# A float32 attention layer on one core: inputs laid out in load order, x loaded transposed, scores of two head pairs at a time, high and low parts as neighbours

## Chip, cores and metric

One core of a Trainium2 chip runs the whole kernel. The metric is the device time of one execution in microseconds; for the kernel before it is the median of three runs, 153.05 (151.89 to 153.78). The host's rearranging of the arrays, ahead of the launch, is outside that time in both kernels.

## The reference

One layer (DEPTH = 1) of attention with a gate, then a root-mean-square norm, in float32, for 256 positions, 16 heads of 64 and a width of 1024. There is one key block of 256 positions, so the block selection of the reference never selects anything, and what is computed is causal attention with a linear distance penalty:

```python
h = rms_norm(x, norm_g)                       # x: 1 x 256 x 1024
q, k, v, gate = split(h @ w_in, 4)            # w_in: 1024 x 4096
s = q @ k.T * 64 ** -0.5 - slope[head] * (t_query - t_key)
s = where(t_key <= t_query, s, -inf)
o = softmax(s) @ v
x = x + (o * silu(gate)) @ w_out              # w_out: 1024 x 1024
return rms_norm(x, final_g)
```

## The kernel before

**Three products for one.** TensorE's fast float32 form (fp32r) keeps fewer bits, so every large product is made of three: each operand a is split into a high part (ACT copies it to fp32r) and a low part (DVE subtracts the high part from a), and high x high, low x high and high x low are added up in one PSUM bank. PEld in the profile is PE's loading of the weight that each matmul has.

**Stages.** The rows of x are in two blocks of 128 (m = 0, 1), the width in eight slices of 128 (k). `w_in` comes in pieces of 512 KB through four buffers, and its columns are projected in parts, in the order of the table `PARTS` (line 28): first half of v, then q, k, gate parts of 256 columns, among them the second half of v as the tenth part, and `w_out` last in eight pieces. A part of q, k or gate holds two head pairs; it takes 8 slices x 2 pairs x 3 matmuls of 256 columns. A part of v takes 8 x 2 x 3 of 512 columns. The norm's factor for each row (`rstd`) is not put into x but into the results, when they leave PSUM.

**The opening** (lines 172 to 179 and 501 to 640). SP issues half a row block of x, the first weight piece in two halves, half of the other row block, and so on. PE transposes x by a product with an identity (`x_tr`, line 519), ACT or DVE evacuate it with the gain into high parts (`x_evac`, line 523), DVE makes the low parts, and the 48 matmuls of the first half of v follow (`run_first`, line 594). Five matmuls on zeros (`warm`, line 496) fill PE before data are there; they wait for a memset on DVE. The 16 tables of the distance penalty (`make_bias`, line 211) are made 7 on DVE and 9 on ACT. Squares of x are summed on ACT (`square`, line 504) between the evacuations, and POOL raises them to the power -0.5 (line 514).

**Attention** (`fiber_pair`, line 317), for each of the 8 head pairs: 12 score matmuls of 64 rows into two PSUM banks, one for each head; for both query blocks DVE adds the penalty and takes the row's maximum in one operation (line 360), ACT takes the exponential with the sums; DVE scales by the reciprocal; PE transposes the probabilities, ACT and DVE split them (`pth`, `ptl`); three matmuls of 512 columns and three of 256 multiply them with the high and low v of both heads of the pair (`vh`, `vl`); DVE multiplies by the gate (line 433), ACT and DVE split the result (`oh`, `ol`).

**What sets the order.** All engines' instructions stand in the order in which Python writes them. A planner (`Plan`, line 53) keeps an estimated clock for each engine with costs for each kind of operation; the projections are written in a loop, and after every matmul `fill` (line 261) may add the splitting of a weight piece, and `side` (line 292) may add a step of one of the "fibers" (a pair's attention, an evacuation) whose inputs are due by the planner's clock. Eight PSUM banks are handed out by `take` and `give`; a projection of two pairs takes two. DMAs of weights are issued on SP as soon as a buffer's low part has been made.

**The end.** Out of the output projection the two row blocks come one after the other; each is added to x, squared, scaled by its factor on ACT and DVE, and leaves in two DMAs on SP (lines 722 to 752).

Of the kernel before, what the change touches and what calls it, by code (L numbers as in the profile page):

```python
# [13 lines left out]
P = 128  # L14
S = 256
# [12 lines left out]
PARTS = [("v", 0), ("q", 0), ("k", 0), ("g", 0), ("q", 1), ("k", 1), ("g", 1), ("q", 2), ("k", 2), ("v", 1),  # L28
         ("q", 3), ("k", 3), ("g", 2), ("g", 3)]
# [4 lines left out]
NKB = 3  # L34
# [8 lines left out]
WARM = 4  # L43
SPREAD = 200.0
WARM2 = 1
NB_DVE = 7
NB_ACT = 3
COLD = 6800.0
NL = 4
# [27 lines left out]
def trunk(ctx: ExitStack, tc, x, norm_g, w_in, w_out, fin_g, out):  # L77
# [9 lines left out]
    qp = ctx.enter_context(tc.tile_pool(name="qp", bufs=4))  # L87
    khp = ctx.enter_context(tc.tile_pool(name="khp", bufs=NKB))
    zp = ctx.enter_context(tc.tile_pool(name="zp", bufs=3))
# [4 lines left out]
    def mm(o, a, b, start, stop, n, dep=0.0):  # L94
        nc.tensor.matmul(o, a, b, start=start, stop=stop)  # L95
        return plan.mm(n, dep)
# [39 lines left out]
    g8 = const.tile([NK, P], F32, name="g8")  # L136
    nc.scalar.dma_start(g8, norm_g.rearrange("(a b) -> a b", b=P))

    x_at = [[0.0, 0.0], [0.0, 0.0]]
    w32, whi, wlo, w_at, w_ready = {}, {}, {}, {}, {}  # L140
    dma = [1680.0]

    def load_x(m, h):
        nc.sync.dma_start(xs[m][:, h * CW:(h + 1) * CW], x[0, m * P:(m + 1) * P, h * CW:(h + 1) * CW])  # L144
        dma[0] += 728.0
        x_at[m][h] = dma[0] + LAT

    def piece_src(i):

        if i < N_IN:  # L150
            kind, j, h = PIECES[i]
            w = CW if kind == "v" else GW
            r = KP * GW // w * P
            return w_in[h * r:(h + 1) * r, COL[kind] + j * w:COL[kind] + (j + 1) * w].rearrange("(a p) n -> p a n", p=P)
        k = i - N_IN
        return w_out[k * P:(k + 1) * P, :].rearrange("p (a n) -> p a n", n=CW)

    def load(i, parts=1, dep=0.0):
        if i >= N_PIECES:
            return  # L160
        w32[i] = w32p.tile([P, KP * GW], F32, name="w32")
        src = piece_src(i)
        a = src.shape[1]
        dst = w32[i].rearrange("p (a n) -> p a n", a=a)
        for u in range(parts):
            us = slice(u * a // parts, (u + 1) * a // parts)
            nc.sync.dma_start(dst[:, us, :], src[:, us, :])  # L167
        s = max(dma[0], dep)
        w_at[i] = [s + LAT + 1456.0 * (u + 1) / parts for u in range(parts)]
        dma[0] = s + 1456.0  # L170

    load_x(0, 0)
# [601 lines left out]
```

## Time and profile before

| | |
|---|---|
| median of 3 runs | 153.05 us |
| profiled execution, its own time | 154.04 us |
| its span, first to last instruction | 152.3 us |
| instructions | 2760 |
| granted TensorE clock, mean | 0.990 |
| DMA moved | 23.78 MB, mean 156 GB/s |

A row of the timeline is: start, duration, engine, line of the kernel, operation, what it writes and reads with the shape, how often it is repeated there, and in brackets the idle time before it and what ended that. A row of a window is: the window, its length, then for each engine the busy time and the number of instructions, the granted clock, the share of the DMA engines' time, and GB/s. A group's row is: what it is, the number, the busy time, the mean in ns of one, and the idle time ahead. Durations of matmuls overlap, so the distance of starts tells what one costs. The profiled execution lies 1.0 us above the median.

### The profile page before, as it was taken

Reading aid. Unit: us, or ns where it says so; the run is one execution under the profiler, and the core shown is the slowest. Engines: PE = TensorE matmul, PEld = TensorE weight load, DVE = VectorE, ACT = ScalarE, POOL = GpSimd, SP = SyncE. Lnnn points to the kernel's source line nnn. Section 1 sums busy time; section 2 is a strip of 40 time slices with the busy share of each in tenths; the row PEclk is TensorE's granted clock in tenths of the full one; section 3 lists DMA queues with packets and bytes.
Section 4 is the critical chain, followed back from the end, with each engine's and each line's share of the span. In section 5 each row is a group of like instructions: output and inputs, shape, how many; then the busy total and the mean of one; then the engine's idle time right before and its main releaser. Section 6 shows DMA issues by size and latency. Waiting matters only on the chain.

```text
span 152.3 us, 2760 instructions
## 1 busy us (share of the span) xinstructions
PE 143.6 (94%) x1008; PEld 129.7 (85%) x1008; DVE 118.7 (78%) x294; ACT 89.6 (59%) x199; POOL 4.1 (3%) x13
## 2 busy tenths in 40 slices
PE   6699999999999999999999999999999999999940
PEld 3388789999999998999997879999899988888830
DVE  5574897596899989898987799767686999674880
ACT  6375997546697443975744878464296493331231
POOL 3000010000000000000000000000000000000210
PEclk9999999999999999999999999999999999999995
DMA  4999479969704454231747605486430406100033
GB/s 142 260 359 338 137 206 265 340 176 279 241 27 138 138 180 158 80 123 31 264 146 210 201 1 154 132 285 235 167 138 4 138 0 229 46 2 4 11 127 138
DMA packets 17390, 23.78 MB, mean 156 GB/s; under 512 B 856, under 2 KB 13408, under 8 KB 17376
## 3 DMA queue, kind: packets, MB, share of 16 engines
q1 hardware_dynamic: 17216, 23.07, 47.1%
q10 hardware_dynamic: 160, 0.53, 1.4%
q8 instruction: 8, 0.13, 0.4%
q14 instruction: 6, 0.05, 0.1%
HBM read 22.55 MB, written 1.05 MB: 155 GB/s over the span
## 4 chain that ended last, share of the span: by engine, by line
PE 87%; DMA 4%; issue 3%; DVE 1%; SPq 1%; POOL 1%; ACT 0%; POOLq 0%
PE bank L95 78%; PE bank L99 5%; PE bank L343 4%; DMA x<-in_x 4%; POOL fr L745 1%; SPq L167 1%; DVE bias L736 0%; ACT bias L747 0%; POOLq L770 0%; DVE x L734 0%; SPq L144 0%; DVE fms L736 0%
## 5 line engine op out<-in xcount | busy, mean ns | idle before, releaser
L95 PE MATMUL bank<-xl,whi 128*128 128x256 f32 x192 | 55.0, 287 | 0.0
L106 ACT ACTIVATE whi<-w 128x1024 fp32r<-128x1024 f32 (+1 forms) x43 | 41.4, 978 | 23.0 <-PE bank L95 9.4
L95 PE MATMUL bank<-xh,wlo 128*128 128x256 f32 x192 | 54.8, 286 | 0.0
L95 PE MATMUL bank<-xh,whi 128*128 128x256 f32 x192 | 54.8, 285 | 0.0
L247 DVE TENSOR_TENSOR wlo<-w,whi 128x1024 fp32r<-128x1024 f32 (+1 forms) x43 | 47.6, 1122 | 8.7 <-ACT whi L106 8.6
L95 PEld LDWEIGHTS bank<-xl,whi 128*128 128x128 f32 x192 | 36.2, 188 | 0.3
L95 PEld LDWEIGHTS bank<-xh,whi 128*128 128x128 f32 x192 | 36.2, 189 | 0.2
L95 PEld LDWEIGHTS bank<-xh,wlo 128*128 128x128 f32 x192 | 36.2, 189 | 0.1
L106 ACT ACTIVATE pr<-st,mx 128x256 f32<-128x256 f32 (+1 forms) x32 | 14.1, 443 | 7.2 <-DVE mx L360 7.2
L95 PE MATMUL bank<-whi,xh 128*128 128x512 f32 x32 | 13.0, 442 | 0.3 <-ACT whi L106 0.3
L95 PE MATMUL bank<-whi,xl 128*128 128x512 f32 x32 | 12.6, 431 | 0.0
L95 PE MATMUL bank<-whi,oh 128*128 128x512 f32 (+1 forms) x35 | 12.6, 359 | 0.0
L95 PE MATMUL bank<-whi,ol 128*128 128x512 f32 (+1 forms) x35 | 12.6, 359 | 0.0
L95 PE MATMUL bank<-wlo,oh 128*128 128x512 f32 (+1 forms) x35 | 12.6, 359 | 0.0
L95 PE MATMUL bank<-wlo,xh 128*128 128x512 f32 x32 | 12.3, 425 | 0.0
L99 PE MATMUL bank<-ident,pr 128*128 128x128 f32 x48 | 12.2, 273 | 0.0
L106 ACT ACTIVATE pth<-bank 128x384 fp32r<-128x384 f32 x16 | 7.8, 488 | 6.9 <-PE bank L99 6.7
L468 DVE TENSOR_TENSOR z<-bank,rows 128x256 f32<-128x256 f32 x24 | 9.5, 422 | 2.7 <-PE bank L95 2.5
L360 DVE CUSTOM_DVE_ANT_0 st<-bank,bias 128x256 f32<-128x256 f32 (+1 forms) x32 | 9.7, 352 | 0.2
L406 DVE TENSOR_TENSOR ptl<-bank,pth 128x384 fp32r<-128x384 f32 x16 | 8.6, 551 | 1.6 <-ACT pth L106 1.5
L433 DVE TENSOR_TENSOR og<-bank,sg 64x256 f32<-64x256 f32 x16 | 6.7, 420 | 2.5 <-PE bank L95 2.2
L95 PEld LDWEIGHTS bank<-whi,xh 128*128 128x128 f32 x32 | 6.5, 204 | 2.3 <-ACT whi L106 0.8
(87 smaller groups left out, 196.0 us busy)
## 6 DMA issues: line engine op xcount, KB each, us to landing
w<-in_moba_w_in SPq DMA_DIRECT2D x28, 512.0 KB, 4.0
w<-in_moba_w_out SPq DMA_DIRECT2D x8, 512.0 KB, 3.3
w<-in_moba_w_in SPq DMA_DIRECT2D x8, 256.0 KB, 5.6
x<-in_x SPq DMA_DIRECT2D x4, 256.0 KB, 5.4
out<-bias SPq DMA_DIRECT2D x2, 320.0 KB, 2.3
gf<-in_final_norm_g ACTq DMA_DIRECT2D x1, 512.0 KB, 6.0
out<-bias SPq DMA_DIRECT2D x2, 192.0 KB, 1.9
g<-in_moba_norm_g ACTq DMA_DIRECT2D x1, 4.0 KB
```

The lines of the kernel that those rows point to most:

```text
L95: nc.tensor.matmul(o, a, b, start=start, stop=stop)
L99: nc.tensor.transpose(o, a, ident)
L106: nc.scalar.activation(o, i, fn, scale=scale, **kw)
L167: nc.sync.dma_start(dst[:, us, :], src[:, us, :])
L247: nc.vector.tensor_sub(wlo[i][:, c], w32[i][:, c], f32(whi[i][:, c]))
L343: nc.tensor.matmul(bs[a]["t"][:, c], u[rr, m * P:(m + 1) * P], w[rr, 0:c.stop - c.start], start=jj == 0, stop=jj == 2)
L360: nc.vector.tensor_tensor_reduce(st[:, a, c0:c1], ps, bt, scale=-1.0, scalar=BIG, op0=ALU.add, op1=ALU.min, accum_out=mx[:, cc:cc + 1])
L406: nc.vector.tensor_sub(lo[:, a], pv, f32(hi[:, a]))
L433: nc.vector.tensor_mul(og[rr, :], po[rr, a, :], sg[rr, p, :])
L468: nc.vector.tensor_mul(z, ps, rows8 if kind == "q" else rows)
L745: nc.gpsimd.tensor_tensor(r, ms[:, ns - 1:ns], mhalf, op=ALU.pow)
```

## The change

**Loads.** The host puts all that is loaded but the final gain into one array, `laid`, in the order in which it is fetched (`LAID`), every piece contiguous. x is in it twice: transposed (`("x", k0, k1)`, into the tile `head` with the gain ahead of it, which later holds the gate `sg`), and by rows (`("t", m)`) after the fifth weight piece. The first pieces are: gain and slice 0 of x (132 KB) on SP, the first half of weight piece 0 (256 KB) and slice 1 of x (128 KB) on ACT's queue, the second half on SP, and then on SP two slices of x (256 KB) and a weight piece in two halves, three times over. Transposes of x are gone. The sums of squares come in a fiber (`fiber_norm`) once the rows are there, after the first half of v.

**Opening.** The zero operand of the warming matmuls is a constant that POOL writes at the very start; there are seven in a row, before the first weights. All 16 penalty tables are made on POOL.

**Evacuations.** A part of q, k or gate is projected into one bank for both pairs and evacuated as 512 columns, with high and low part in one tile; the factor one half of the gate comes from a third copy of the row factors, so that the sums need not be doubled.

**Scores** are issued for two pairs as one block, four banks at a time. For the first query block, kh and kl are one 256-column operand, so that the sum's last addition is one of DVE (line 387 after).

**Products with v.** High and low v of a head stand side by side as one weight of 128 columns, for each head by itself: three matmuls of 256 columns for a head. ACT copies the half that comes from the low v, DVE adds the pieces and then multiplies by the gate.

**Order of parts and end.** The second half of v now comes after the last q and k. For the first row block the last slice alone is done by column group, its factor is applied on ACT in two steps, the second among the steps of the next block, and it leaves in two DMAs of 256 KB.

```diff
-PARTS = [..., ("q", 2), ("k", 2), ("v", 1), ("q", 3), ("k", 3), ("g", 2), ("g", 3)]
+PARTS = [..., ("q", 2), ("k", 2), ("q", 3), ("k", 3), ("v", 1), ("g", 2), ("g", 3)]
+LAID = [("x", 0, 1), ("w", 0, 0, 2), ("x", 1, 2), ("w", 0, 1, 2)]
+for c in range(1, NK // 2):
+    LAID += [("x", 2 * c, 2 * c + 2), ("w", c, 0, 2), ("w", c, 1, 2)]
+LAID += [("w", NK // 2, 0, 1)] + [("t", m) for m in range(NM)]
+LAID += [("w", i, 0, 1) for i in range(NK // 2 + 1, N_PIECES)]
...
+    load_xt(0, 1)
+    load(0, 2, part=0, queue=nc.scalar)
+    load_xt(1, 2, nc.scalar)
+    load(0, 2, part=1)
+    for c in range(1, NK // 2):
+        load_xt(2 * c, 2 * c + 2)
+        load(c, 2)
...
+    def make_bias(h):
         slope = -(2.0 ** (-8.0 * (h + 1) / H))
+        nc.gpsimd.tensor_scalar(bias[:, h, :], dist, slope, 0.0, op0=ALU.mult, op1=ALU.add)
...
+    def scores(p):
+        while not all(u in at_k and u in at_q for u in (p, p + 1)):
+            yield poll()
...
+        both = [b0] + [take_now() for _ in range(3)]
...
+        steps = [(1, u, jj) for u in (p, p + 1) for jj in range(3)] + [(0, u, jj) for jj in range(2) for u in (p, p + 1)]
+        for m, u, jj in steps:
...
+            terms = ((qh, (0, 1)), (ql, (0,))) if m == 0 else ((qh, (0,)), (qh, (1,)), (ql, (0,)))
...
+                nc.tensor.matmul(o, q[rr, m * P:(m + 1) * P], kt[rr, ts[0]:ts[-1] + 1, 0:n],
+                                 start=jj == 0, stop=jj == len(terms) - 1, skip_group_check=True)
...
+                if m == 0:
+                    nc.vector.tensor_add(st[:, a, c0:c1], bs[a]["t"][:, S + P:S + 2 * P], bt)
...
-        nc.vector.tensor_scalar(rs, rs, 2.0, None, op0=ALU.mult)
...
-        for jj, (u, w) in enumerate(((hi, vh), (hi, vl), (lo, vh))):
-            mm(po, w[0][:, cols], u[:, :, 0:2, :], jj == 0, False, 2 * S)
...
+        for a in range(2):
+            po = two[a]["t"]
+            w = [vv[m][:, 2 * p + a].rearrange("p t n -> p (t n)") for m in range(NM)]
+            for t in range(2):
+                mm(po[:, 0:S], w[0], pt[:, a, 0:2, t, :], t == 0, False, S)
+            yield 0
+            r = mm(po[:, P:P + S], w[1], pt[:, a, 2].rearrange("p t n -> p (t n)"), False, True, S)
...
-            nc.vector.tensor_mul(og[rr, :], po[rr, a, :], sg[rr, p, :])
+            e = act(cs[rr, :], po[DH:P, 0:S], AF.Copy, S, r, True)
...
+            nc.vector.tensor_add(og[rr, :], po[0:DH, 0:S], cs[rr, :])
...
+            nc.vector.tensor_add(og[rr, P:S], po[0:DH, S:S + P], og[rr, P:S])
...
+        nc.vector.tensor_mul(og, og, sg[:, p, :])
...
+        def x_lo(k):
+            nc.vector.scalar_tensor_tensor(xl[k], sg[:, k, :], gT[:, k:k + 1], f32(xh[k]),
+                                           op0=ALU.mult, op1=ALU.subtract)
...
+        for c in range(NK // 2):
+            for a in range(2):
+                x_hi(2 * c + a, "act" if c else "dve")
+                split_hi(2, a)
+                x_lo(2 * c + a)
...
+                split_lo(2, a)
+            if c == 0:
+                load_x(0)
+                load_x(1)
...
+        def fiber_norm():
+            for m in range(NM):
+                for h in range(2):
+                    yield x_at[m]
+                    d = square(m, h)
+                yield d
+                d_root = root(m, d)
...
-            acc = [take_now() for _ in range(2)]
+            acc = [take_now() for _ in range(2 if kind == "v" else 1)] * (1 if kind == "v" else 2)
```

**How it moves instructions.** PE in the opening; `bank` are PSUM banks, `xh`, `xl`, `whi`, `wlo` high and low parts of x and of the weights, L498 and L543 the warming matmuls, L99 transposes. Before:

```order
L498 MATMUL bank_98<-oh 128x512 x4
L567 MATMUL bank_97<-ident,g_101 128x8
L99 MATMUL bank_91<-ident,x_99 128x128 x2
L99 MATMUL bank_92<-ident,x_99 128x128 x2
L498 MATMUL bank_98<-oh 128x512
L95 MATMUL bank_95<-whi,xh 128x512
L95 MATMUL bank_95<-whi,xl 128x512
L99 MATMUL bank_91<-ident,x_100 128x128 x2
L99 MATMUL bank_92<-ident,x_100 128x128 x2
```

After:

```order
L543 MATMUL bank_101<-const-float32-0.0 128x512 x7
L107 MATMUL bank_98<-whi,xh 128x512
L107 MATMUL bank_99<-whi,xh 128x512
L107 MATMUL bank_98<-whi,xl 128x512
L107 MATMUL bank_99<-whi,xl 128x512
L107 MATMUL bank_98<-wlo,xh 128x512
L107 MATMUL bank_99<-wlo,xh 128x512
```

Both row blocks (banks 98 and 99) now follow each other slice by slice, with no transposes between. PE at the first scores, the two heads of a pair in turn (L343, L354 are score matmuls). Before, the first pair's and what stands behind it:

```order
L343 MATMUL bank_91<-kl,qh 128x256
L343 MATMUL bank_95<-kl,qh 128x256
L343 MATMUL bank_91<-kh,ql 128x256
L343 MATMUL bank_95<-kh,ql 128x256
L343 MATMUL bank_91<-kh,qh 128x128
L343 MATMUL bank_95<-kh,qh 128x128
L343 MATMUL bank_91<-kl,qh 128x128
L343 MATMUL bank_95<-kl,qh 128x128
L343 MATMUL bank_91<-kh,ql 128x128
L343 MATMUL bank_95<-kh,ql 128x128
L95 MATMUL bank_96<-xl,whi 128x256
L343 MATMUL bank_97<-kh,qh 128x256
```

After, the end of the block of 20:

```order
L354 MATMUL bank_95<-k,q 128x256
L354 MATMUL bank_99<-k,q 128x256
L354 MATMUL bank_100<-k,q 128x256
L354 MATMUL bank_101<-k,q 128x256
L354 MATMUL bank_95<-k,q 128x256
L354 MATMUL bank_99<-k,q 128x256
L354 MATMUL bank_100<-k,q 128x128
L354 MATMUL bank_101<-k,q 128x128
L354 MATMUL bank_95<-k,q 128x128
L354 MATMUL bank_99<-k,q 128x128
L107 MATMUL bank_97<-xh,whi 128x256
```

The projection matmul between the two pairs is gone, and the three 128-column steps of a pair (each for both heads) have become one of 256 columns and one of 128. ACT around the sums of squares (`ss`); the tiles w_187 and w_209 before, w_187 and w_201 after are the fifth and sixth weight pieces. Before:

```order
L106 ACTIVATE whi<-w_116 128x512 x2
L106 ACTIVATE sg,ss<-x_99 128x512
L106 ACTIVATE sg,ss<-x_100 128x512
L106 ACTIVATE whi<-w_187 128x1024
L106 ACTIVATE whi<-w_209 128x1024
```

After:

```order
L118 ACTIVATE whi<-w_119 128x512
L118 ACTIVATE whi<-w_187 128x1024
L118 ACTIVATE head,ss<-x_102 128x512 x2
L118 ACTIVATE head,ss<-x_103 128x512 x2
L666 DMA gf<-in_fin_g 128x1024
L118 ACTIVATE whi<-w_201 128x1024
```

All four sums now stand between the fifth and the sixth piece.

More of the change, by code (lines that the diff above doesn't have):

```diff
@@ L148, in piece_src, with fetch @@
[L148 to L158, printed above, removed]
+    dma = [1600.0]
+    def fetch(o, seg, queue=None, dep=0.0):
+        n = P * WIDTH[seg]
+        (queue or nc.sync).dma_start(o, laid[START[seg]:START[seg] + n].rearrange("(p n) -> p n", p=P))
+        dma[0] = max(dma[0], dep) + n / 90.0
+        return dma[0] + LAT
@@ L159, in load, with load_x, load_xt @@
+    def load_x(m):
+        x_at[m] = fetch(xs[m], ("t", m))
+    def load_xt(k0, k1, queue=None):
+        o = head[:, (NK + k0 * S if k0 else 0):NK + k1 * S]
+        at = fetch(o, ("x", k0, k1), queue)
+        for k in range(k0, k1):
+            xt_at[k] = at
+    def load(i, parts=1, dep=0.0, part=None, queue=None):
         if i >= N_PIECES:
             return
[L161 to L172, printed above, removed]
-    load(0, 2)
-    load_x(1, 0)
-    load(1, 2)
-    load_x(0, 1)
-    load_x(1, 1)
-    for i in range(2, NL):
-        load(i, 2)
+        if not part:
+            w32[i] = w32p.tile([P, KP * GW], F32, name="w32")
+            w_at[i] = []
@@ L414, in fiber_pair @@
         while True:
-            b = take(keep[0])
+            b = take(keep[0] + 1)
             if b is not None:
@@ L565, in trunk @@
             b["busy"] = True
-        first, second, both = slice(0, P), slice(P, S), slice(0, S)
-        nc.tensor.transpose(banks[6]["t"][:, :NK], g8, ident[:NK, :NK])
-        d = plan.mm(NK, 3480.0)
-        nc.vector.tensor_copy(gT, banks[6]["t"][:, :NK])
-        dve(NK, d)
-        r = [x_tr(0, k) for k in range(4)][1]
-        warm(WARM2)
-        for _ in x_evac(0, first, r, "dve"):
-            pass
-        for _ in hi():
-            pass
-        split_lo()
+        for c in range(NK // 2):
+            for a in range(2):
+                x_hi(2 * c + a, "act" if c else "dve")
+                split_hi(2, a)
+                x_lo(2 * c + a)
+                whi_at.setdefault(c, []).append(w_ready[c][a])
+                split_lo(2, a)
+            if c == 0:
+                load_x(0)
+                load_x(1)
         def term(m, k, jj):
@@ L598, in run_first @@
                     return
+                warm_to(term(*u))
                 todo.remove(u)
@@ L701, in trunk @@
             for c0, c1 in GROUPS[m]:
+                until(lambda: any(not b["busy"] for b in banks))
                 accs[m, c0] = take_now()
@@ L726, in trunk @@
             ms = sm.tile([P, 4], F32, name="fms")
+            late = NK - 1 if m == 0 else NK - 4
+            for k in range(NK - 4, late):
+                for c0, c1 in GROUPS[m]:
+                    until(lambda: k in at_o)
+                    plan.pe = max(plan.pe, at_o[k])
+                    outmm(k, m, c0, c1, accs[m, c0]["t"][:, :c1 - c0])
             for u, (c0, c1) in enumerate(GROUPS[m]):
@@ L729, in trunk @@
                 o = accs[m, c0]["t"][:, :c1 - c0]
-                for k in range(NK - 4, NK):
+                for k in range(late, NK):
                     until(lambda: k in at_o)
```

361 lines of the change are left out of this document (176 added, 185 removed).

## The prediction, made before the changed kernel ran

> **What bounds the kernel now.** I read the page's busy times and slices, then windows by stage, then the opening as a timeline, then the rows of single operations.
>
> ```profile
> PE 143.6 (94%) x1008; PEld 129.7 (85%) x1008; DVE 118.7 (78%) x294; ACT 89.6 (59%) x199; POOL 4.1 (3%) x13
> PE   6699999999999999999999999999999999999940
> ```
>
> PE is the bound, and not just on average: nine tenths or more in every slice from the third to the one before the tail. Two windows, cut where the second projection starts (22.05) and where the output projection starts (120.04), say it more sharply.
>
> ```profile
> 22.05:120.04 97.99, 97.99 (x796) 1.00 0.52 164
> 120.04:146.30 26.26, 26.26 (x146) 1.00 0.20 71
> ```
>
> The columns are the window, its length, PE busy, granted clock, DMA share and GB/s. PE is never idle for 124.25 us at a granted clock of 1.00. So a microsecond is won only by fewer or cheaper matmul slots there, by reaching 22.05 sooner, or by shortening what follows the last matmul; DVE and ACT cost nothing until they make PE wait. How long a slot is:
>
> ```profile
> 117.78 0.28 PE L95 MATMUL bank<-xh,wlo 128*128 128x256 f32 x1
> 117.90 0.28 PE L95 MATMUL bank<-xh,whi 128*128 128x256 f32 x1
> ...
> 129.62 0.39 PE L95 MATMUL bank<-whi,oh 128*128 128x512 f32 x1
> 129.85 0.39 PE L95 MATMUL bank<-wlo,oh 128*128 128x512 f32 x1
> ```
>
> The starts, not the durations, give it: 0.12 us (0.119 over longer rows) for 256 columns, 0.233 for 512.
>
> **The opening.** Before 22.05 lie the 48 matmuls of the first value projection: 48 x 0.233 = 11.2 us at full speed, so some 10 us are lost ahead of and among them.
>
> ```profile
> 4.80 0.63 ACT L106 ACTIVATE whi<-w 128x512 fp32r<-128x512 f32 x1 [1.12 <-DMA w<-in_moba_w_in]
> 6.77 0.63 ACT L106 ACTIVATE whi<-w 128x512 fp32r<-128x512 f32 x1 [1.34 <-DMA w<-in_moba_w_in]
> 7.66 1.09 PE L99 MATMUL bank<-ident,x 128*128 128x128 f32 x4 [0.95 <-DMA x<-in_x]
> 8.97 0.63 PE L95 MATMUL bank<-whi,xl 128*128 128x512 f32 x1
> 9.40 1.05 PE L95 MATMUL bank<-wlo,xh 128*128 128x512 f32 x2
> 11.96 1.38 PE L99 MATMUL bank<-ident,x 128*128 128x128 f32 x8
> 13.65 0.62 PE L95 MATMUL bank<-whi,xh 128*128 128x512 f32 x2
> 22.05 0.28 PE L95 MATMUL bank<-xh,whi 128*128 128x256 f32 x1
> ```
>
> PE had to wait for both row blocks of x and transpose them: at 7.66 it had stood idle for a block still on its way. From 8.97 to 9.40 a 512-column matmul takes 0.43, half speed, and two take 1.05; at 13.65 two take 0.62, full speed. So PE stayed slow for some 4.3 us of unbroken work (7.66 to 11.96), although the granted clock reads 1.00 throughout.
>
> [...]
>
> How fast data came, with the same chip and similar packets:
>
> ```profile
> 0.00:3.00 3.00, 1.55 (x4) 1.17 (x4) 1.50 (x7) 1.64 (x3) 1.39 (x9) 1.00 0.39 128
> 3.00:5.00 2.00, 2.00 (x8) 1.21 (x6) 1.28 (x7) 0.88 (x4) 0.00 (x0) 1.00 0.81 216
> 5.00:8.00 3.00, 1.76 (x5) 0.87 (x5) 1.72 (x4) 1.06 (x2) 0.00 (x0) 1.00 0.96 281
> 8.00:12.00 4.00, 4.00 (x13) 3.12 (x12) 2.81 (x7) 3.00 (x8) 0.00 (x0) 1.00 1.03 366
> 12.00:15.00 3.00, 3.00 (x17) 2.68 (x16) 1.19 (x3) 2.06 (x5) 0.00 (x0) 1.00 1.04 342
> ```
>
> The last column times the length, added up: 0.38 MB by 3 us, 0.82 by 5, 1.66 by 8, 3.12 by 12, 4.15 by 15. Each load here is 256 KB, 0.262 MB. The second weight half ends the third of them, at 0.79 MB, on the curve at 4.9, but used at 6.77; the first ends the second, at 0.52 MB, 3.6, used at 4.80: a lag of 1.2 to 1.9, 1.5 taken.
>
> **The change part by part.** *Opening.* The 16 transposes of x and that of the gain go, x comes transposed in pieces between the weights, and the row-wise x comes after the fifth weight piece. The first weight half now ends at 0.40 MB (0.135 of x and gain, 0.262): 3.1 on the curve, 4.6 with the lag, 5.2 after its 0.63 on ACT. From there 48 matmuls: 4.3 us at half speed are 10 of them, the other 38 take 8.9, so the second projection starts at 18.4. The data would allow about the same: the third k slice needs 1.31 MB (0.131 of x, 0.262 of weight, 0.262 of x and 0.262 of weight more), 6.7 + 1.5 = 8.2, some 1.2 for high and low part, and from 9.5 six slices of 1.4 give 17.9. I take 18.2, that is -3.85. The bounds: lag 1.2 and warm early gives 16.7, lag 1.9 with slow ACT and DVE 20.5.
>
> ACT and DVE must keep up with 1.4 us for each k slice:
>
> ```profile
> 9.59 1.16 ACT L106 ACTIVATE whi<-w 128x512 fp32r<-128x512 f32 x2
> 10.54 1.28 DVE L247 TENSOR_TENSOR wlo<-w,whi 128x512 fp32r<-128x512 f32 x2
> 13.81 0.88 DVE L537 SCALAR_TENSOR_TENSOR xl<-bank,gT,xh 128x256 fp32r<-128x256 f32 x2 [1.99 <-PE bank L95]
> 17.08 0.64 ACT L106 ACTIVATE sg<-x 128x512 f32<-128x512 f32 x1
> 18.31 2.01 ACT L106 ACTIVATE whi<-w 128x1024 fp32r<-128x1024 f32 x2
> ```
>
> Per slice DVE has half of 1.28 and of 0.88, 1.08 us, ACT half of 1.16 and about as much as DVE for x, 1.0. Both fit, because the 16 bias tables leave them (7 on DVE, 9 on ACT) for POOL.
>
> *A wait that is added there.* The sums of squares now wait for the late x, and ACT takes its work in order: behind the four squares stands the high part of the sixth piece. The second x block ends at 4.72 MB, 16.7 on the curve, 18.2 with the lag; its two squares (17.08 to 18.31 in the rows, 1.23) end at 19.4, the high part (half of 2.01) at 20.4, the low part on DVE (two halves, 1.28) at 21.7. PE wants it 26 slots of 0.119 after 18.2, at 21.3. So +0.4, and -3.45 for the whole opening.
>
> *Values times probabilities.* High and low of v stand side by side as one 128-column weight, so a pair takes six matmuls of 256 columns instead of three of 512 and three of 256: 8 x 3 x (0.233 - 0.119) = -2.75. These are slots of the kind measured, so it is nearly certain.
>
> *Scores of two pairs together.*
>
> ```profile
> 36.86 0.28 PE L95 MATMUL bank<-xh,whi 128*128 128x256 f32 x1
> 37.08 0.39 PE L343 MATMUL bank<-kh,qh 64*128 64x256 f32 x2
> ...
> 37.53 0.23 PE L343 MATMUL bank<-kh,qh 64*128 64x128 f32 x2
> 37.59 0.28 PE L343 MATMUL bank<-kl,qh 64*128 64x128 f32 x2
> ...
> 37.91 0.39 PE L95 MATMUL bank<-xl,whi 128*128 128x256 f32 x1
> ...
> 39.06 0.38 PE L95 MATMUL bank<-xh,wlo 128*128 128x256 f32 x1
> 39.28 0.28 PE L95 MATMUL bank<-xh,whi 128*128 128x256 f32 x1
> ```
>
> Both heads of a pair run at once. From 36.86 to 39.28 are 2.42 us less three ordinary slots, 2.06 for two pairs, of which every change between the two kinds costs 0.1 at both ends. Now there is one such change in and out, six double slots of 0.117, two of 0.117 with kh and kl as one 256-column operand, and two of 128: 1.5. Four times -0.5 is -2.0; if the short ones fill a whole slot, -1.4. I take -1.9.
>
> *What DVE and ACT get in return.* DVE adds the third score term (16 of 128 columns) and joins the halves of the output (16 of 64x128 and 8 of 128x256, besides the 16 of 64x256 that were there); ACT copies 16 halves. Wide evacuations, the absent doubling of the sums and the tables give some back. By these rows
>
> ```profile
> L360 DVE CUSTOM_DVE_ANT_0 st<-bank,bias 128x128 f32<-128x128 f32 x16 | 4.2, 284 | 0.0
> ...
> 37.00:84.00 47.00, 47.00 (x397) 44.55 (x395) 41.73 (x113) 29.41 (x71) 0.00 (x0) 1.00 0.47 146
> ```
>
> the short ones are 0.28 each (32) and the 8 long ones 0.42: 12.4 us at most, 6.2 of them for the four pairs between 37 and 84, before what is given back. DVE (the third busy time) has 47 - 41.7 = 5.3 us free there, and PE's part gets 2.3 shorter, so at worst 3.2 us come through. What hides this is the projections' PE work between the scores and the products, most of all the second value projection, now behind the last scores, which gives pairs 6 and 7 another 11 us of PE work to hide in. I take +0.7 for waits; bounds 0 and, if 3.2 come through in both halves, 6.
>
> *Tail.* The second row block's steps after the last matmul are the same ones, 6.0 us; moving the first block's scaling and its two output DMAs forward on SP lies under matmuls. 0.
>
> **Sum.** -3.45 - 2.75 - 1.9 + 0.7 = -7.4. The profiled execution took 154.04 (span 152.3 and 1.74 around it), which gives 146.6; it lies 1.0 above the median of the runs, 153.05, so I forecast 153.05 - 7.4 = 145.65, said as 145.7. All bounds together are -10.1 to +0.7, and the likeliest case by itself 142.5 to 148.
>
> **Rivals.** *POOL and DVE block each other in the opening (0.14).* POOL's power at the end shows it:
>
> ```profile
> 142.09 0.69 DVE L746 TENSOR_TENSOR bias<-x,gf 128x512 f32<-128x512 f32 x1
> 142.26 0.93 POOL L745 TENSOR_TENSOR fr<-fms,mhalf 128x1 f32<-128x1 f32 x1 [122.50 <-DVE fms L736]
> ...
> 147.30 0.42 DVE L746 TENSOR_TENSOR bias<-x,gf 128x256 f32<-128x256 f32 x1
> 147.47 0.66 POOL L745 TENSOR_TENSOR fr<-fms,mhalf 128x1 f32<-128x1 f32 x1 [4.28 <-DVE fms L736]
> ...
> 1.56 0.40 POOL L188 TENSOR_SCALAR_AFFINE_SELECT dist<-dist 128x256 f32<-128x256 f32 x1
> ```
>
> Both ended 0.41 us after DVE's operation on two SBUF inputs (142.78 and 147.72): POOL waited for DVE. The opposite, DVE waiting for POOL, no row shows. The nearest POOL row, 0.40 for 128x256, makes the 16 tables 6.4 us, from 1.96 to 8.4 alone and to some 12 in turns with DVE. If DVE waits as well, each of its ten operations in that time may lose up to 0.4: 4 us, of which one is hidden while PE is slow. That is 3 more, less the 0.4 of the wait for the sixth piece, which then falls away: 148.3. [...]
>
> *The opening gains nothing (0.08).* Landing lags grow with two queues, or the squares hold ACT longer. For it speaks 5 to 8 us at 281 GB/s with a share of 0.96; against it that PE no longer needs both row blocks of x. 153.05 - 4.65 + 0.7 = 149.1.
>
> *Banks run out (0.06), slower.* Scores now take four of the eight PSUM banks at once and a pair's product two. If PE stands at the next instruction that needs a bank until DVE has drained four (four times 0.42 and four times twice 0.28, 3.9, and up to 1.7 of a low part and an evacuation ahead of them, 5.6), four groups cost up to 4 x 5.6 less what PE has in its own bank; at 2.6 each, 10.4: 155.4 (145.7 without its 0.7, and 10.4). It makes the kernel slower from 2.0 us a group, a quarter of the gain without waits. Against it: the projections now need one bank, not two, and PE did not wait once in 124 us by this planner.
>
> *Scores save nothing*, since the 64-row matmuls of two pairs don't overlap as one pair's do, is in the likeliest case's range: 147.6.
>
> **Chances.** The forecast 0.72, the rivals as given. Range 142.3 to 150.0: below, early warmth and no waits; above, the first two rivals. A change of 2%, 3.06 us, is about what a measurement here can tell: faster than that 0.88, within 0.07, slower 0.05.
>
> **What would show it.** The first 256-column projection matmul near 18 (not 22.05), with PE at half speed until about 9.5; six slots of 0.119 for each pair's product; one block of 20 score matmuls in about 1.35 us, four times; PE without gaps after 22, but for one of about 0.4 near 21, put down to whi or wlo. Wrong would be: DVE gaps in the first 12 us put down to POOL, PE gaps behind the scores put down to DVE, or a longer stretch from the last matmul to the end than 6 us.

## The result, and the profile after

The changed kernel takes 143.25 us (median of 4 runs, 142.99 to 144.65), the kernel before 152.57 on the same footing (4 runs, 151.89 to 153.78): a ratio of 0.940, 95% interval 0.931 to 0.949. The forecast was 145.7, 2.4 too high; the range, 142.3 to 150.0, holds it. Both profiled executions lie above the medians of their kernels, by 1.5 and 1.4 us, and the ratios in this document leave out executions more than 1.5% above the fastest of their kernel. The two profiled executions, cut at the start of the second projection and at the start of the last matmul:

| us | before | after | difference | forecast |
|---|---|---|---|---|
| up to the second projection | 22.05 | 17.84 | -4.21 | -3.85 |
| from there to the last matmul's start | 123.98 | 118.93 | -5.05 | 0.4 - 2.75 - 1.9 + 0.7 = -3.55 |
| from there to the end of the span | 6.27 | 6.13 | -0.14 | 0 |
| around the span | 1.74 | 1.75 | 0 | 0 |
| sum | 154.04 | 144.65 | -9.39 | -7.4 |

The forecast's +0.4 for the late x stands in the second row, since that wait was expected near 21.3, behind the start of the second projection at 18.2.

From the page of the changed kernel, the busy times and PE's row of slices:

```profile
PE 135.8 (95%) x977; PEld 125.1 (88%) x977; DVE 123.3 (86%) x285; ACT 94.7 (66%) x198; POOL 13.6 (10%) x29
PE   7899999999999999999999999999999999999930
```

PE is still the bound, and DVE is closer to it: 86%, not 78%. From its timeline, first the opening, then one block of scores, two rows among the products with v, and the end:

```profile
0.76 3.33 PE L543 MATMUL bank<-const-float32-0.0 128*128 128x512 f32 x7 [0.76 <-PEq L811]
3.94 0.63 ACT L118 ACTIVATE whi<-w 128x512 fp32r<-128x512 f32 x1 [1.01 <-DMA w<-in_laid]
4.03 0.57 DVE L580 SCALAR_TENSOR_TENSOR xl<-head,xh 128x256 fp32r<-128x256 f32 x1
4.62 1.22 PE L107 MATMUL bank<-whi,xh 128*128 128x512 f32 x2 [0.54 <-DVE xl L580]
...
8.21 0.94 PE L107 MATMUL bank<-whi,xl 128*128 128x512 f32 x2
8.98 0.62 PE L107 MATMUL bank<-wlo,xh 128*128 128x512 f32 x2
...
13.28 0.47 DVE L580 SCALAR_TENSOR_TENSOR xl<-head,xh 128x256 fp32r<-128x256 f32 x1
...
16.77 0.63 ACT L118 ACTIVATE head<-x 128x512 f32<-128x512 f32 x1
...
17.84 0.28 PE L107 MATMUL bank<-xh,whi 128*128 128x256 f32 x1
...
32.85 0.28 PE L107 MATMUL bank<-xh,wlo 128*128 128x256 f32 x1
33.06 1.40 PE L354 MATMUL bank<-k,q 64*128 64x256 f32 x20
34.38 0.38 PE L107 MATMUL bank<-xh,whi 128*128 128x256 f32 x1
34.60 0.28 PE L107 MATMUL bank<-xl,whi 128*128 128x256 f32 x1
...
110.24 0.28 PE L107 MATMUL bank<-pt,vv 128*128 128x256 f32 x1
110.36 0.28 PE L107 MATMUL bank<-xh,whi 128*128 128x256 f32 x1
...
136.77 0.28 PE L107 MATMUL bank<-xh,ol 128*128 128x256 f32 x1
```

The first real matmul starts at 4.62 (5.2 forecast), PE turns from two matmuls in 0.85 us to two in 0.47 within the row at 8.21, at about 8.9 (9.5), and the 48 matmuls then end at 17.84 without a gap. The 20 score matmuls take 34.60 - 32.85, less two ordinary slots of 0.119: 1.51, where two pairs took 2.06. A product's matmul costs 0.12, an ordinary slot. The last square of x starts on ACT at 16.77; a start after 18.2 was forecast.

Windows of the changed kernel, cut at the same places (columns as in the prediction: window, length, then busy time and number of PE, PEld, DVE, ACT, POOL):

```profile
60.00:90.00 30.00, 30.00 (x242) 28.78 (x241) 28.50 (x72) 20.84 (x47) 0.00 (x0) 1.00 0.43 143
90.00:113.00 23.00, 23.00 (x179) 21.19 (x178) 21.67 (x56) 18.58 (x43) 0.00 (x0) 1.00 0.50 167
...
121.00:136.80 15.80, 15.80 (x90) 13.66 (x88) 13.07 (x26) 6.35 (x13) 0.93 (x1) 1.00 0.04 15
sum 118.96, PE 118.96 PEld 112.25 DVE 109.17 ACT 80.88 POOL 2.44; mean PE 19.83 PEld 18.71 DVE 18.20 ACT 13.48 POOL 0.41
```

PE is busy for all of the 118.96 us, DVE for 109.17. So PE's slots alone made up that stretch, and DVE had 9.8 us to spare in it, 4.2 of them in its two ends (before 30 and after 121). Whether that is a margin is the question of the fourth group of experiments.

### The profile page after: what moved, and what is told of

It reads as the page before. It is cut to its first block, busy times and chain, and to the rows that moved or that the text cites. A ratio compares the mean times of both kernels' runs of the same rounds, so it can differ in the third digit from the quotient of the medians.

```text
span 142.9 us, 2686 instructions
## 1 busy us (share of the span) xinstructions
PE 135.8 (95%) x977; PEld 125.1 (88%) x977; DVE 123.3 (86%) x285; ACT 94.7 (66%) x198; POOL 13.6 (10%) x29
## 2 busy tenths in 40 slices
DMA packets 8077, 24.81 MB, mean 174 GB/s; under 512 B 896, under 2 KB 1280, under 8 KB 8064
## 4 chain that ended last, share of the span: by engine, by line
PE 88%; DVE 3%; issue 3%; DMA 2%; POOL 1%; ACT 1%; POOLq 0%
PE bank L107 81%; PE bank L111 4%; PE bank L354 4%; DMA head<-in_laid 2%; DVE x L756 1%; POOL fr L770 1%; DVE bias L760 1%; ACT bias L777 1%; POOLq L818 0%; DVE bias L765 0%; DVE xl L580 0%; DVE xh L576 0%; DVE fms L732 0%; DVE fms L760 0%
## 5 line engine op out<-in xcount | busy, mean ns | idle before, releaser
L251 DVE TENSOR_TENSOR wlo<-w,whi 128x1024 fp32r<-128x1024 f32 (+1 forms) x43 | 48.7, 1139 | 5.2 <-ACT whi L118 5.1
L770 POOL TENSOR_TENSOR fr<-fms,mhalf 128x1 f32<-128x1 f32 x2 | 1.6, 798 | 115.7 <-DVE fms L760 115.7
L118 ACT ACTIVATE pt<-bank 128x384 fp32r<-128x384 f32 x16 | 7.8, 487 | 3.2 <-PE bank L111 3.1
L107 PE MATMUL bank<-pt,vv 128*128 128x256 f32 x48 | 9.9, 281 | 0.0
L434 DVE TENSOR_TENSOR pt<-bank,pt 128x384 fp32r<-128x384 f32 x16 | 8.7, 551 | 0.7 <-ACT pt L118 0.7
L220 POOL TENSOR_SCALAR bias<-dist 128x256 f32<-128x256 f32 x16 | 8.6, 536 | 1.0
```

The lines of the kernel that those rows point to most:

```text
L107: nc.tensor.matmul(o, a, b, start=start, stop=stop, skip_group_check=True)
L118: nc.scalar.activation(o, i, fn, scale=scale, **kw)
L220: nc.gpsimd.tensor_scalar(bias[:, h, :], dist, slope, 0.0, op0=ALU.mult, op1=ALU.add)
L251: nc.vector.tensor_sub(wlo[i][:, c], w32[i][:, c], f32(whi[i][:, c]))
L434: nc.vector.tensor_sub(lo, pv, f32(hi))
L770: nc.gpsimd.tensor_tensor(r, ms[:, ns - 1:ns], mhalf, op=ALU.pow)
```

## The experiments

All are edits of the changed kernel, and each was timed beside the kernel before on the same chip. "Full speed" is when PE's 512-column matmuls go from 0.43 to 0.23 us, read from the distances of the starts (the turn, in what follows); "to the last" runs from the second projection's start to the last matmul's start.

| run | median us (runs) | ratio to before, 95% | full speed | second projection | to the last |
|---|---|---|---|---|---|
| changed kernel | 143.25 (4) | 0.940, 0.931-0.949 | 8.9 | 17.84 | 118.93 |
| the same again | 143.19 (4) | 0.934, 0.930-0.939 | 5.8 | 16.37 | 118.98 |
| ten zero matmuls | 143.58 (4) | 0.939, 0.932-0.947 | by 5.2 | 16.45 | 119.13 |
| no zero matmuls | 144.56 (4) | 0.944, 0.938-0.951 | 9.1 | 17.79 | 118.99 |
| tables as constants | 146.1 (4) | 0.955, 0.949-0.961 | by 6.3, 11.2 | 19.27 | 118.99 |
| tables on DVE and ACT | 144.06 (4) | 0.943, 0.936-0.950 | 10.2 | 18.41 | 118.92 |
| weights not laid out | 144.74 (4) | 0.942, 0.936-0.948 | 9.7 | 18.39 | 118.92 |
| old order of parts | 143.72 (5) | 0.936, 0.929-0.942 | 5.2 | 17.47 | 119.78 |
| scores pair by pair | 144.94 (4) | 0.942, 0.935-0.949 | 6.7 | 16.78 | 120.35 |
| third term twice | 148.32 (4) | 0.965, 0.958-0.971 | by 4.5 | 16.24 | 124.30 |
| both additions twice | 153.64 (10) | 1.007, 1.002-1.012 | 6.7 | 16.79 | 128.35 |
| third term left out | 143.52 (4) | 0.938, 0.933-0.943 | by 4.6 | 16.23 | 119.04 |
| nine zeros, other end | 144.35 (6) | 0.943, 0.939-0.947 | about 5.0 | 16.26 | 118.99 |

### When PE turns fast

```diff
         warm_to(3480.0)
+        warm(4)
```

> Ten matmuls on zeros in the changed kernel's opening instead of seven; all else stays. There the seven ran from 0.76 to about 4.1, PE then stood 0.54 us, the first real matmul came at 4.62, and PE turned fast at 8.8, 4.2 us after 4.62. Theory: PE turns fast after some 4.2 us without a gap, and the gap of 0.54 threw the zeros' work away. Ten fill it: first real matmul at about 5.1, full speed from then on, the second projection starts at 16.3 to 16.6 instead of 17.84, and if the pieces keep up the whole takes 1.2 us less, about 142. Rival: work on zeros does not count, or the turn comes at a fixed time: the first real matmul is 0.4 later for nothing, the second projection starts at 18.2, and the whole is 0.4 longer.

From the timeline of this run:

```profile
0.76 4.60 PE L543 MATMUL bank<-const-float32-0.0 128*128 128x512 f32 x10 [0.76 <-PEq L812]
5.15 0.68 PE L107 MATMUL bank<-whi,xh 128*128 128x512 f32 x2
...
16.45 0.28 PE L107 MATMUL bank<-xh,whi 128*128 128x256 f32 x1
```

The first real pair already starts the next one 0.52 later, and nearly all others 0.47: the theory's numbers (5.1, 16.3 to 16.6). Work on zeros counted in this execution: full speed by 5.2. Yet the median, for which about 142 was expected, did not fall below the changed kernel's, so the profiled execution there seems not to be its usual one. The converse:

```diff
-                nc.tensor.matmul(banks[7]["t"], zero.to_broadcast([P, P]), zero.to_broadcast([P, CW]),
-                                 start=True, stop=True)
```

> No matmuls on zeros at all in the changed kernel; the order of everything else is kept. Theory: interrupted work is thrown away, so the seven zeros gave nothing; PE turns fast 4.2 us after its first real matmul as before, the second projection starts at 17.8 (at most 0.3 later) and the time stays at 143.3. Rival: the zeros brought the turn forward in part; without them PE stays slow longer and the second projection starts 0.5 to 1.7 later.

The profiled execution fits the theory to 0.05 us (17.79). The median is 1.3 above the changed kernel's, which would fit the rival, although the two ratios' intervals overlap. Both would be so if the changed kernel itself came out differently from execution to execution. It was run again, unedited:

> The changed kernel itself, unedited, for one more profiled execution and as the neighbour of the next one. By the runs so far PE turns fast at the end of a window of some 3.4 us that runs on its own clock, if PE stood less than about 0.5 us in it: theory: this execution's turn falls anywhere from 5 to 10 us, the second projection starts between 16.3 (fast from about 5) and 18.4, and from there to the start of the last matmul it takes 118.9 again. Rival: the place of the turn is set by the program; the turn is at 8.8 to 8.9 and the second projection starts at 17.8 again.

Its timeline:

```profile
4.50 1.22 PE L107 MATMUL bank<-whi,xh 128*128 128x512 f32 x2 [0.42 <-ACT whi L118]
5.53 0.73 PE L107 MATMUL bank<-whi,xl 128*128 128x512 f32 x2
...
16.37 0.28 PE L107 MATMUL bank<-xh,whi 128*128 128x256 f32 x1
```

Full speed from about 5.8 on, not 8.9, with the same program; the second projection starts 1.47 earlier, and the whole took 143.24 instead of 144.65. Everything behind is equal (118.98). So the turn is not set by unbroken work counted from its start. The reading that fits these runs is that it comes at the end of a window with a clock of its own (3.41 us, below), if PE stood little enough in it (0.42 to 0.48 us in three runs, below). In the runs with seven zeros, without the two whose pause ahead of the first real matmul was longer (0.88 with the weights not laid out, 2.22 with constant tables, below), that pause was 0.32 to 0.54, and the turn came anywhere from before 4.5 to 10.2.

The length of the window shows in the moments at which the granted clock changed, which the traces keep. In the run with constant tables these are 4.40, 7.81 and 11.23; in the one with the third term twice 3.69, 133.40 and 136.81. The steps are 3.41 us and, from 3.69 to 133.40, 38 times 3.41. In the kernel before the clock changed at 12.66 and, behind the last matmul, at 149.19, 40 steps later; in the changed kernel at 8.88 and 142.00, 39 steps later.

How much idle time a window may hold is not settled. Of the windows of 3.41 us that end at the turn or just one window ahead of it, those with 0.42 (2.34 to 5.75, repeated run), 0.45 (3.22 to 6.64, both additions twice) and 0.48 (0.27 to 3.69, third term twice) without a matmul counted as busy; those with 0.50 (3.34 to 6.75, tables on DVE and ACT) and 0.54 (2.05 to 5.47, changed kernel) did not. But in the kernel before an earlier one with 0.28 (2.42 to 5.83), which has transposes in it, did not count either.

Whether the zeros help on average is less sure. All four executions without them (143.87 to 144.65) took longer than seven of the eight of the unedited kernel, but not on the same chip. Ten instead of seven won nothing in the median.

### POOL and DVE

```diff
-        nc.gpsimd.tensor_scalar(bias[:, h, :], dist, slope, 0.0, op0=ALU.mult, op1=ALU.add)
+        nc.gpsimd.memset(bias[:, h, :], slope)
```

> The 16 penalty tables are filled by POOL with a constant, which reads nothing from SBUF, instead of being computed from the distance tile (so the output has neither penalty nor causal mask). Theory: DVE's operations on two SBUF inputs and POOL's reading ones hold each other up: without the reading, the low parts of x take 0.47 us from the start (0.57 to 0.61 with the tables) and those of the weight halves 0.68 (0.79 to 0.88), while the start of the second projection stays within 0.3 of 17.84, since PE's own slots pace the opening. Rival: the stretch comes from something else in the opening (transfers landing), and the low parts stay at 0.57 to 0.61 and 0.79 to 0.88 until 11.5. A third: the stretch was on the path, and the second projection starts 1 us or more earlier.

From the timeline of this run:

```profile
1.91 4.12 POOL L220 MEMSET bias<- 128x256 f32 x16
...
3.42 2.75 DVE L576 TENSOR_SCALAR xh<-head 128x256 fp32r<-128x256 f32 x1 [2.55 <-DMA head<-in_laid]
...
6.21 0.48 DVE L580 SCALAR_TENSOR_TENSOR xl<-head,xh 128x256 fp32r<-128x256 f32 x1
6.32 0.71 PE L107 MATMUL bank<-whi,xh 128*128 128x512 f32 x2 [2.22 <-DVE xh L576]
6.61 0.69 DVE L251 TENSOR_TENSOR wlo<-w,whi 128x512 fp32r<-128x512 f32 x1
...
8.01 1.05 PE L107 MATMUL bank<-whi,xh 128*128 128x512 f32 x2
```

As the theory has it, the low parts take 0.48 and 0.69 once POOL no longer runs; but they never met a memset, so that part proves less than it was meant to. What met them was the first high part of x, a DVE operation with one tile as input: 2.75 us instead of 0.35, ended just after POOL's last memset at 6.03. By these times sixteen writes in a row, 0.26 each, held DVE off for their whole row; it is one execution. None of the three cases expected that. PE's pause of 2.22 us was followed by half speed from 7.8 to 11.2 (the two matmuls at 8.01 take 0.86 from start to start), and both together put the second projection 2.9 us later than in the repeated run (19.27 against 16.37). In the changed kernel the tables stretch DVE's low part of x only from 0.47 to 0.57 (rows at 13.28 and 4.03), at most 0.61. The next run takes them away from POOL:

```diff
-        for h in range(H):
-            make_bias(h)
...
+                for h in (2 * (2 * c + a), 2 * (2 * c + a) + 1):
+                    make_bias(h, "dve" if h % 2 and h > 1 else "act")
```

> The 16 tables go back to DVE (7) and ACT (9), one or two of them with each of the eight slices of the opening; POOL makes none. Theory: what POOL's tables took from DVE (0.1 to 0.2 on each operation) is nearly what a table costs there, 0.29; each slice then needs about 1.44 us on DVE and on ACT, PE needs 1.4, so the second projection starts at 17.9 to 18.6, and the whole is 0 to 0.8 us longer. Rival: taking the tables off DVE and ACT carried much of the opening's gain, and the second projection starts 2 to 3.5 us later than 17.84, as the 2.0 us of tables on DVE and 2.8 on ACT push the slices.

The second projection starts at 18.41, inside the theory's 17.9 to 18.6, and even that is the clock's doing: PE turned at 10.2, not 8.9, and 1.3 us at half speed are worth the 0.57. DVE's low parts take 0.48 and 0.69 here from the start (at 4.05 and 4.58), so it was POOL's products that stretched them (0.57 to 0.61 and 0.79 to 0.88 in the changed kernel); which of their operands matter, no run separates. Neither place for the tables holds PE up.

### The loads

```diff
-            w_at[i].append(fetch(w32[i][:, u * n:(u + 1) * n], ("w", i, u, parts), queue, dep))
+            (queue or nc.sync).dma_start(dst[:, us, :], src[:, us, :])
```

> All weight pieces come out of the original arrays again, in packets of one row of a column block (1 or 2 KB), in the same order and at the same places of the queue; x stays in the host's layout. Theory: in the opening PE's slots, not the data, set the pace from the second slice on; only the first weight half is late by the difference of the rates (128 against 107 GB/s were no slower ahead of 3 us, 216 against 355 from 3 to 5), so the second projection starts 0 to 0.6 later than in the changed kernel at the same clock history, and later stages do not change. Rival: 281 instead of 335 GB/s from 5 to 8 and 366 instead of 407 from 8 to 12 pass through to PE: 3.15 MB are needed for the last slice, they come 1.2 to 1.5 us later, and the second projection starts that much later.

Windows of this run (the last column is GB/s; in the changed kernel the same windows have 335 and 407):

```profile
5.00:8.00 3.00, 3.00 (x7) 2.44 (x8) 2.96 (x6) 2.53 (x5) 2.71 (x5) 1.00 1.02 364
8.00:12.00 4.00, 4.00 (x15) 3.18 (x15) 4.00 (x7) 3.77 (x9) 2.96 (x5) 1.00 1.05 383
```

And its page's row of packets, 8077 of them in the changed kernel:

```profile
DMA packets 17805, 24.81 MB, mean 173 GB/s; under 512 B 896, under 2 KB 13568, under 8 KB 17792
```

More than twice the packets bring 364 and 383 GB/s: the rate hardly falls, so packet size is not why the kernel before got 281 here. The first matmul starts 0.34 later (4.96), the pause before it is 0.88, and the turn comes at 9.7. The second projection starts at 18.39, 0.55 later than in the changed kernel and inside the theory's 0 to 0.6; the rival's 1.2 to 1.5 is not there. So the gain of the opening is not in the contiguous weights. That it lies in what PE no longer has to wait for, both row blocks of x and their transposes, is left over by this run, not shown by one that puts them back.

### What DVE can still take

```diff
-PARTS = [..., ("q", 2), ("k", 2), ("q", 3), ("k", 3), ("v", 1), ("g", 2), ("g", 3)]
+PARTS = [..., ("q", 2), ("k", 2), ("v", 1), ("q", 3), ("k", 3), ("g", 2), ("g", 3)]
```

> The second half of v goes back ahead of the last q and k parts in the changed kernel; nothing else is edited. Theory of the prediction: that half, now behind the last scores, is the cover for the softmax of pairs 6 and 7; with the old order the last scores come 11 us later, and DVE, busy 21.4 of 22.7 us between 90 and 112.7, is late for the output projection: PE stands 1.5 to 4 us ahead of its last slices, put down to DVE, and the whole takes that much longer, 145 to 147. Rival: the planner spreads DVE's work so that the order of the parts does not matter; PE stands under 0.3 us and the time is 143.3 within half a microsecond.

PE's waits in this run (who waited for whom, us in total, how often, the longest):

```profile
PE bank L107 <- ACT whi L118: 1.3, 2, 1.0
...
PE bank L107 <- DVE ol L479: 0.4, 1, 0.4
```

One wait of 0.4 for DVE within the output projection, at 129.3, and 0.85 more to the last matmul (the 1.3 are in the opening, where a slice of x landed late). The rival was nearer: the order of parts is worth under a microsecond, and is not the cover that the prediction named first. Then DVE's new work twice, all of it, half of it, and half of it left out:

```diff
-                    nc.vector.tensor_add(st[:, a, c0:c1], bs[a]["t"][:, S + P:S + 2 * P], bt)
+                    for _ in range(2):
+                        nc.vector.tensor_add(st[:, a, c0:c1], bs[a]["t"][:, S + P:S + 2 * P], bt)
...
-            nc.vector.tensor_add(og[rr, :], po[0:DH, 0:S], cs[rr, :])
+            for _ in range(2):
+                nc.vector.tensor_add(og[rr, :], po[0:DH, 0:S], cs[rr, :])
```

> Two of the operations that the change gave DVE are done twice, with the same result: the addition of the third score term (16 of 0.28 us) and that of the output's halves (16 of 0.41), 11.1 us more on DVE, some 9.7 of it between 30 and 113 us, and the planner is told. In the changed kernel DVE is free there for 2.6 + 1.5 + 1.3 = 5.4 us, and PE does not wait. Theory: what the change gave DVE just fits, and from the point where DVE has no free time PE waits one for one: 3 to 6 us more, with PE gaps behind scores and products put down to DVE. Rival: the free time elsewhere (3.1 us after 113, 1.3 between 18 and 30) and the buffers take most of it: under 1.5 us more.

> Only the addition of the third score term is done twice (16 of 0.28, 4.5 us more on DVE). Doubling it and the addition of the output's halves, 11.1 us, made the stretch from the second projection's start to the last matmul's start 128.35 instead of 118.93. Theory: up to the output projection DVE has 1.7 us that it can give, and each further one makes PE wait: 2 to 3.5 us more. Rival: there is a margin, of the size of DVE's idle 6.7 us between 18 and 113, and only what goes beyond it counts: under 0.6 us more.

> The addition of the third score term is left out (the product of high q and low k in the first query block is computed and not added): 4.5 us less on DVE. Theory: PE's own slots set the time from the second projection on, so the stretch to the last matmul's start stays at 118.9 within 0.2. Rival: DVE limits as well (it is busy 21.7 of 23 us before the output projection), and the stretch gets 0.5 us or more shorter.

11.1 us more on DVE made the stretch 9.4 longer, 4.5 more made it 5.4 longer, 4.5 less changed it by 0.1. Windows of the run with 4.5 more:

```profile
90.00:113.00 23.00, 23.00 (x176) 21.40 (x176) 22.43 (x59) 18.57 (x42) 0.00 (x0) 1.00 0.50 159
...
128.00:131.00 3.00, 1.34 (x9) 1.03 (x7) 1.71 (x5) 0.76 (x2) 0.00 (x0) 1.00 0.00 0
...
134.00:137.00 3.00, 3.00 (x9) 2.37 (x8) 2.42 (x6) 0.52 (x3) 0.93 (x1) 0.53 0.00 0
```

and its timeline:

```profile
127.44 0.50 PE L107 MATMUL bank<-whi,ol 128*128 128x512 f32 x1 [0.38 <-DVE ol L481]
...
128.71 0.63 PE L107 MATMUL bank<-pt,vv 128*128 128x256 f32 x4
131.97 0.50 PE L107 MATMUL bank<-xh,oh 128*128 128x512 f32 x1 [2.62 <-ACT oh L118]
...
133.50 0.63 PE L107 MATMUL bank<-whi,oh 128*128 128x512 f32 x1
133.93 0.63 PE L107 MATMUL bank<-wlo,oh 128*128 128x512 f32 x1
...
136.87 0.40 PE L107 MATMUL bank<-whi,ol 128*128 128x512 f32 x1
```

Up to 113 PE waits for nothing, although DVE has 22.4 of 23 us filled. The backlog comes out at the end: PE runs out of output projection, does the last products alone at 128.71 and stands 2.62 us until the last pair's result has been through DVE and ACT. That pause then costs again: in the window from 134 the granted clock is 0.53, slots are 0.43 from 133.4 to 136.8, and 3.4 us at half speed are 1.7 lost. 0.38 + 2.62 + 1.7 = 4.7 of the 5.4; the rest is open. The rival, 6.7 us to spare, fell. The theory's 2 to 3.5 us holds for PE's waits, 3.0, and had not counted the clock's 1.7. With both additions twice PE waits 6.6 us of the 9.4, in seven places between 110 and 138, and half speed follows there too, from 129.5 to 132.9. So the changed kernel stands near the edge: of 4.5 us more on DVE about 1.5 are absorbed, of 11.1 about 4.5, and nothing is won by taking off. The planner was told of the added work, so the order of the steps changed with it.

The half-speed window is partly chance. The pause of 2.62 fell so that one window of 3.41 us (129.98 to 133.39) had 1.99 without a matmul; the pause of 0.96 in the opening of the run with the old order of parts was followed by no half speed. Two of the four executions with the third term twice (148.32 and 146.67) have a mean granted clock of 0.997, and a half-speed window alone would take 1.2% off it.

### Scores

```diff
-        steps = [(1, u, jj) for u in (p, p + 1) for jj in range(3)] + [(0, u, jj) for jj in range(2) for u in (p, p + 1)]
+        steps = [s for u in (p, p + 1) for s in [(1, u, 0), (1, u, 1), (1, u, 2), (0, u, 0), (0, u, 1)]]
...
+            if (m, u, jj) == (0, p, 1):
+                plan.pe += 2 * SWITCH
+                yield 0
```

> The scores of two pairs are still started together, but first all of one pair, then an ordinary projection matmul, then all of the other. A block cost 1.51 us beyond ordinary slots, two separate pairs of the kernel before 2.06. Theory: of the 0.55 saved, two more changes between 128-row and 64-row matmuls are 0.2, and the lone short matmul at a pair's end some 0.06 to 0.1; four blocks split this way cost 1.0 to 1.3 us, the last matmul ends 1.0 to 1.3 us later counted from the start of the second projection (119.2 there). Rival: changes between the kinds cost nothing by themselves and the saving is only that of the joined high and low part: under 0.3 us in all.

From this run's timeline, the second block:

```profile
54.81 0.28 PE L107 MATMUL bank<-xh,wlo 128*128 128x256 f32 x1
55.02 0.80 PE L354 MATMUL bank<-k,q 64*128 64x256 f32 x10
55.75 0.38 PE L107 MATMUL bank<-xh,whi 128*128 128x256 f32 x1
56.06 0.80 PE L354 MATMUL bank<-k,q 64*128 64x256 f32 x10
56.80 0.38 PE L107 MATMUL bank<-xl,whi 128*128 128x256 f32 x1
57.02 0.28 PE L107 MATMUL bank<-xh,wlo 128*128 128x256 f32 x1
```

57.02 - 54.81 less three slots of 0.119 is 1.85, against 1.51 together and 2.06 before. So of 0.55 a block, 0.34 is the two changes between the kinds of matmul saved and the pairs' short matmuls side by side, and 0.21 the joined high and low part of k. Four times 0.34 is 1.4; the stretch is 1.42 longer, a little above the theory's 1.3, and the rival's 0.3 fell.

### A version meant to beat both

```diff
+        warm(3)
...
+            nc.vector.scalar_tensor_tensor(z[:, c], y[:, c], r, gf[:, c], op0=ALU.mult, op1=ALU.mult)
-            for c0, c1 in ((cut, D), (CW, cut)):
+            for c0, c1 in ((cut, D - GW), (CW, cut)):
```

> Two edits of the changed kernel. Nine matmuls on zeros instead of seven, so that they end at about 4.7, where the first real operands are ready: PE should turn fast by 7.6 at the latest in every execution, and the second projection start at 16.0 to 16.9. And in the last step the multiplication by the final gain moves behind POOL's power and takes the row factor with it for the last 256 columns, so that POOL no longer waits for a DVE operation on two SBUF inputs: theory: POOL's 0.66 becomes 0.3 to 0.4 and the stretch from the last matmul's start to the end of the span goes from 6.13 to 5.7 or 5.8. Rival for that: the last DMA follows ACT's scaling and not this chain, and the stretch stays at 6.1. Together 0.5 to 1.3 us below the changed kernel's median on the same chip.

Its timeline:

```profile
4.73 0.77 PE L107 MATMUL bank<-whi,xh 128*128 128x512 f32 x2
...
135.25 0.28 PE L107 MATMUL bank<-xh,ol 128*128 128x256 f32 x1
...
136.62 0.55 POOL L771 TENSOR_TENSOR fr<-fms,mhalf 128x1 f32<-128x1 f32 x1 [3.52 <-DVE fms L761]
137.21 0.48 DVE L780 SCALAR_TENSOR_TENSOR bias<-x,fr,gf 128x256 f32<-128x256 f32 x1 [0.66 <-POOL fr L771]
137.92 0.81 SPq L784 DMA_DIRECT2D out<-bias  x2
```

And its last transfer in the list of DMA issues (the last number is us from issue to landing):

```profile
out<-bias SPq DMA_DIRECT2D x1, 320.0 KB, 3.1
```

It lost. The opening did what was expected (16.26). But POOL's power takes 0.55 alone where it took 0.67 behind DVE, so only 0.12 was won there, DVE's longer operation took it back, the first output DMA is issued 2.67 after the last matmul's start (2.52 in the repeated run), and the last transfer lands 3.1 after its issue instead of 2.3: the end is 6.95 instead of 6.15. All six executions were slower than all four of the unedited kernel on that chip. Why the last transfer takes longer to land is open; no run tells.

## Why the prediction was right, and where it was off

**The bound.** Right: only PE's slots, the opening and the end counted; taking 4.5 us off DVE changed nothing.

**Opening, -3.85 forecast for the second projection's start, -4.21 measured.** The mechanism fits (no transposes, first matmul when the first half piece is there), the sizes less. ACT took the first weight half at 3.94, 0.8 behind the 3.1 of the curve, where 1.5 was taken and 1.2 was the least; so the first matmul came at 4.62 and not 5.2, and PE's own count, 18.4, less these 0.58 is 17.8. The step "PE stayed slow for some 4.3 us of unbroken work" was wrong as a rule, and misread by 0.7: the trace of the kernel before has the clock's change at 12.66, not 11.96, at the end of the first window of 3.41 us behind PE's pause of 0.95. In the changed kernel the rule gave the profiled execution's turn nearly (8.9 for 9.5) by luck, because that one happened to turn late; the repeated run turned at 5.8 and gained 1.47 more. The early warmth in the lower of the bounds, 16.7 to 20.5, rests on no row of the kernel before; the repeated run, fast from 5.8, started the second projection at 16.37, below that bound. The kernel before has one trace only, so how much of -4.21 is the chance of two turns stays open.

**The added wait, +0.4: not there.** It rested on the rates of the kernel before, 366 and 342 GB/s after 8 us. Now 407 and 408 came, the late x was there early, and its last square started at 16.77.

**Products, -2.75: right**, 48 slots of 0.12; no run puts the old products back, the size is read from the slots, among which PE never waits. **Scores, -1.9:** the block cost the 1.5 that the rows gave; four times 0.55 is 2.2, and leaning to the smaller saving took 0.3 off.

**Waits, +0.7: none in the changed kernel**, and the reason given was half wrong. The old order of parts costs only 0.85. What spares PE is that DVE's work just fits: the bound of 6 was not idle, since 4.5 us more on DVE cost 5.4. Together these make 0.4 for the opening, 0.4 for the added wait, 0.3, 0.7, and 0.1 for the end: 1.9 of the 2.0 between -7.4 and -9.39.

**Rivals.** POOL and DVE do hold each other up (DVE's low part of x 0.57 beside POOL's tables, 0.47 without; POOL's power 0.67 behind DVE, 0.55 alone), and with constants instead of products the second projection came 2.9 us later, the clock's fall included; with the tables as they are it was 0.1 to 0.2 an operation, not the 0.4 that the rival counted with, and hidden, since PE at 1.4 us a slice was slower than DVE at 1.28 to 1.34. Banks did not run out: no wait behind scores in any run with the change's own work. The reading that POOL's power lost 0.41 to DVE at the end was wrong by the run with the other end; there POOL's power alone took 0.55, so it lost 0.12.

## What to carry to other kernels

Read the clock's history before comparing openings: the same program differed by 1.5 us by the moment at which PE turned fast, so compare stretches behind it. Filling the pause ahead of the first real matmuls brought the second projection of the profiled execution to 16.45, yet the median did not fall (143.58). A stretch in which PE never waits can still be at the edge: DVE had 9.8 us free in the sum, and 4.5 us more work cost 5.4, because the backlog came out in the last pair, where nothing was left to cover it. And a pause late in the kernel can cost twice, by itself and by a half-speed window behind it: 2.62 us and 1.7 with the third term twice.

## What the runs showed of the hardware

- Sixteen POOL memsets of 128x256 in a row (4.12 us, tables as constants) held back a DVE operation of 0.35 us for 2.4 us, to the end of the whole row; POOL's products of the same size (changed kernel) stretched DVE's low part only from 0.47 to 0.57. Why the memsets held it longer, no run shows.
- A PE pause of 2.62 us (third term twice) was followed by half speed from 133.4 to 136.8, beginning 1.4 us after PE had resumed (granted clock 0.53 from 134 to 137).
- Laid out in windows of 3.41 us from the turn, half speed followed the one from 129.98 to 133.39 with 1.99 us without a matmul (third term twice), and did not follow the one from 135.17 to 138.59 with 1.54 (changed kernel, whose last matmul ends at 137.05; the clock fell at 142.00). How much sets it off, no run shows.
- With 8077 packets (changed kernel) instead of 17805 (weights not laid out), the rate was 335 GB/s from 5 to 8 us and 407 from 8 to 12, against 364 and 383.
